# GLA stage of a hybrid decoder layer: queries, keys, decayed keys and outputs turned by VectorE's 32x32 transposes and DMA by way of DRAM instead of TensorE, with head pairs innermost

## The chip, the cores and the metric

The kernel runs on one core of a Trainium2 chip. The metric is the device time of one execution in microseconds. A profile is one execution in which the hardware profiler recorded what each engine did: PE (TensorE; PEld its weight loads), DVE (VectorE), ACT (ScalarE), POOL (GpSimd) and SP, the queue from which this kernel issues its DMAs. Each engine runs its own list of instructions strictly in order and waits on semaphores for the others.

## The reference

One layer over 2048 prompt tokens (and 8x8 sample tokens) of width 1024, in fp32. The change touches the second of its two head groups, gated linear attention (GLA), of 4 heads with keys of 64 and values of 128 columns:

```python
h = rms_norm(x, g_mix_pre)
proj = jnp.einsum('btd,de->bte', h, w_in)
q, k, v, gq, gk, gv, gr, glr = jnp.split(proj, points, axis=-1)
... sliding-window attention of q, k, v -> attn
log_a = log_sigmoid(glr @ w_gk2 + b_gk) / 16          # one decay per token and key column
o, s_new = gla_chunked(gq, gk, gv, log_a, s_init)
o = rms_norm(o, g_gla) * silu(gr)
mix = concat([attn, o]) @ w_out
x = x + rms_norm(mix, g_mix_post)
h = rms_norm(x, g_ffn_pre)
x = x + rms_norm(relu(h @ w_up) ** 2 @ w_down, g_ffn_post)

# gla_chunked, per head, b = running sum of log_a inside a chunk:
#   attn[t, s] = sum_k q[t, k] * 0.125 * exp(b[t, k] - b[s, k]) * k[s, k]     for s <= t
#   o = attn @ v + (q * 0.125 * exp(b)) @ S
#   S = exp(b_last) * S + (k * exp(b_last - b)).T @ v
```

## The kernel before, in words

The program has three parts: the projection and attention of the first head group (to about 308 us), the GLA stage (308 to about 680 us) and the output projection with the MLP (to the end). The change lies in the GLA stage, in `gla(i, gp, og)`, a generator that is run for 16 blocks of 128 tokens. `gp` holds a block's projected queries (columns 0 to 255), keys, values and output gate, tokens on the partitions.

A block is worked off with a hierarchy of levels. For block lengths b of 1 to 64 (`LEVELS`), `before` and `after` hold, with key columns on the partitions and tokens along the free axis, sums of log decays from a sub-block's start and to its end; `level_sums` takes the exponentials for one level (ACT, into `dec`) and then doubles the sub-blocks (two sums on DVE). `weighted` multiplies the left halves' decays with the keys (`XK`) and the right halves' with the queries (`XQ`), on DVE. The matmuls `gl` (levels 0 to 3) and `gh` (levels 4 to 6) take `XK` and `XQ` to the pieces of the attention matrix. `put_level` copies the pieces by mask into `AH` (DVE, COPY_PREDICATED), `put_diagonal` sets the diagonal from the row sums `dg` of queries times keys, and the matrix then stands in `AT`. The state's update is the matmul `ds` of decayed keys `kd` (tokens on the partitions) and values, the state's part of the output the matmuls `o` and `ds` of `qd` and `S`. The `AT` matmuls complete the output of the block.

Key columns must therefore lie on the partitions, while `gp` has tokens there. Four transposes on PE (`gqk`, in `qk_T`) turn queries and keys; a DVE copy (`kt`) and two ACT copies scaled by 0.125 (`qz`, which holds the two heads of a pair in two planes, with zeros in the other head's rows) bring them to SBUF. The decayed keys are computed turned (`kdT`) and brought back by two PE transposes and an ACT copy (`keys_decayed`); in the same PSUM bank, every second block, the low-rank gate input `glr` of two later blocks is turned too. The finished outputs `og` (from `finish_out`: four squares `ojunk` on ACT, a root of the mean `rs_v`, `ors` on DVE and POOL, four products on DVE) are turned by four PE transposes (`ogT`), copied by ACT to `mo` and stored by one DMA to `mix_d`, from where the out projection loads them. The last block's outputs stay in SBUF. Key columns lie as two groups g of 128, group outermost, then tokens.

What sets the order: PE's list is filled with projection matmuls of later blocks (`gproj`, and out-projection matmuls at the end) between the dependent steps; `G_FILL` gives their numbers for the five stretches of a block. `gla` works on the outputs of block i-1 and the decays `z` of block i+1 beside block i. The order on the other engines is fixed when the program is built, by a scheduler that models each engine; `tc.issue_after` adds an edge. So nothing moves aside at run time for an instruction that waits. On SP's list stand also the loads of projection operands (`gxh`, `gxl`), of output-projection weights (`wor`), stores of their split halves (`wo_d` from `wop0`, made on ACT, and `wop1`, made on DVE) and, near the stage's end, loads of these again.

Of the kernel before, what the change touches and what calls it, by code (L numbers as in the profile page):

```python
# [12 lines left out]
F32 = mybir.dt.float32  # L13
# [28 lines left out]
NL = len(LEVELS)  # L42
S_LEVELS = (1, 2, 4)
# [32 lines left out]
G_FILL = (34, 14, 16, 8, 20)  # L76
# [76 lines left out]
def hybrid_step_kernel(ctx: ExitStack, tc: tile.TileContext, I, O):  # L153
# [43 lines left out]
    sm_d = dpool.tile([P, NFC, 2, 2 * NS], F32, name="sm_d")  # L197
    new_d = {name: dpool.tile([NS, P], F32, name=f"new_{name}") for name in "kv"}
# [777 lines left out]
    def log_decays(i, z, t, gt, out):  # L976
        for g in range(2):
            te.matmul(z[:, g], wgk[:, i % 2, g * P : (g + 1) * P], gt[:, : z.shape[2]], start=True, stop=True)
        nc.scalar.activation(t, z, AF.Abs)
        nc.scalar.activation(t, t, AF.Exp, scale=-1.0)  # L980
        if out is not None:
            nc.scalar.activation(out, t, AF.Ln, bias=1.0)
        return z
# [55 lines left out]
    XK = sp.tile([P, NL, 2, P], F32, name="XK")  # L1039
    XQ = sp.tile([P, NL, 2, 2, P // 2], F32, name="XQ")  # L1040
    sgs, prs = places("sg", [P, 512]), places("pr", [P, 256])
    qds = places("qd", [P, 2, P])
    decs = places("dec", [P, NL + 1, 2, P])
    befores, afters = places("before", [P, 2, P]), places("after", [P, 2, P])
    kts = places("kt", [P, 2, P], 2)
    qz = sp.tile([P, 2, 2, P], F32, name="qz")
    zts, kdTs = places("zt", [P, 2, P], 2), places("kdT", [P, 2, P])
# [18 lines left out]
    for u in range(2):  # L1066
        nc.vector.memset(S[u], 0.0)
    nc.gpsimd.memset(qz, 0.0)
# [6 lines left out]
    def decays(i, n, before, kind="d"):  # L1075
# [6 lines left out]
        t = next(zts)[:, :, :n]  # L1082
        if i:
            z = log_decays(i, bank([P, 2, n], kind, f"z_{i}"), t, gt, t)
        else:
            nc.gpsimd.tensor_copy(gt, f32(glrT_first))
            z, e = z0
            nc.scalar.activation(t, e, AF.Ln, bias=1.0)
        nc.vector.scalar_tensor_tensor(before, z, 0.0, t, op0=ALU.min, op1=ALU.subtract)

    def gate(i, gp, n):
# [6 lines left out]
        nc.vector.scalar_tensor_tensor(t[:n], gr, 0.0, t[:n], op0=ALU.min, op1=ALU.subtract)  # L1098
# [4 lines left out]
        engine.tensor_tensor(t4, t4, ggla[:n].unsqueeze(1).to_broadcast([n, 4, P]), op=ALU.mult)  # L1103
        return t

    def qk_T(i, gp, n, kind="d"):
# [6 lines left out]
        kt, q = (next(kts), qz) if n == P else (s_kt, s_qz)  # L1113
        nc.vector.tensor_copy(kt, pt[:, :, 0, :])
        for r, rr in enumerate(half_of):
            nc.scalar.activation(q[rr, r], pt[rr, :, 1, :], AF.Copy, scale=0.125)
        return kt

    def halves(t, b):

        v = t.rearrange("p g (m s b) -> p s g m b", s=2, b=b)
        return v[:, 0], v[:, 1]

    def pairs(t, b, s):
        lead = "p r" if len(t.shape) == 4 else "p"
        t = t.rearrange(f"{lead} g (m s b) -> {lead} (g m) s b", s=2, b=b)
        return t[..., s, :]

    def weighted(xk, xq, dec, kt, q, l, b):
# [4 lines left out]
        out = xq[:, l].rearrange("p r g (m b) -> p r (g m) b", b=b)  # L1134
        nc.vector.tensor_tensor(out, dr.unsqueeze(1).to_broadcast(list(out.shape)), pairs(q, b, 1), op=ALU.mult)

    def keys_decayed(after, kt, kdT, n, kind, kd, pair=0):
# [4 lines left out]
        pk = bank([P, 3, P], kind, f"kdT_{n}")  # L1142
        for g in range(2):
            te.transpose(pk[:n, g, :], kdT[:, g, :], ident)
        ranks = ranks_T(pair, pk[:, 2]) if pair else None
        nc.scalar.activation(kd[:n], pk[:n, :2].rearrange("p g k -> p (g k)"), AF.Copy)
        if pair:
            nc.scalar.activation(glrT[pair % 2], ranks, AF.Copy)

    def level_sums(before, after, dec, l, b):  # L1150
# [3 lines left out]
        left, right = halves(dec[:, l], b)  # L1154
        (bl, br), al = halves(before, b), halves(after, b)[0]
# [3 lines left out]
        nc.vector.tensor_tensor(al, al, br[..., b - 1 :].to_broadcast(list(al.shape)), op=ALU.add)  # L1159
        nc.vector.tensor_tensor(br, br, bl[..., b - 1 :].to_broadcast(list(br.shape)), op=ALU.add)  # L1160

    def put_level(at, gm, mk, b):

        dst = halves(at, b)[1]
# [3 lines left out]
    def put_diagonal(i, at, gp, n):  # L1168

        pr = next(prs)  # L1170
        with tc.issue_after(put[0].ins) if 0 < i < NB else nullcontext():
            nc.vector.scalar_tensor_tensor(pr[:n], gp[:n, 0:256], 0.125, gp[:n, 256:512], op0=ALU.mult, op1=ALU.mult)
# [5 lines left out]
    def finish_out(i, og_src, sg, n, kind):  # L1178
# [3 lines left out]
        for h in range(4):  # L1182
            nc.scalar.activation(junk[:n], og_src(h), AF.Square, accum_out=ssq[:n, h : h + 1])
# [12 lines left out]
        for _ in range(S_WAIT[0] if i == NB else 1):  # L1196
            yield 44, True
        pt = bank([P, 4, P], kind, f"ogT_{i}")
# [11 lines left out]
    def decayed(i):  # L1210

        before, after = next(befores), next(afters)
        yield from decays(i, P, before, "d" if i else "b")
# [3 lines left out]
    def gla(i, gp, og=iter(())):  # L1217
# [6 lines left out]
        kt = qk_T(i, gp, P, "c")  # L1224
        dec = next(decs)
        following = decayed(i + 1) if i < NB - 1 else iter(())
        yield G_FILL[0] + 3 * (i == 1) if i else G_FIRST_FILL, True
        deque(og, 0)
        put_diagonal(i, AH, gp, P)
        for l, b in enumerate(LEVELS):  # L1230
# [5 lines left out]
            if l == NL - 1:  # L1236
                kd = next(kds)
                pair = i // 2 + 1 if i % 2 == 0 and i < NB - 2 else 0
                turned = keys_decayed(after, kt, next(kdTs), P, "e", kd, pair)
                nc.scalar.activation(dec[:, NL], before, AF.Exp, scale=1.0 / 16)  # L1240
            weighted(XK, XQ, dec, kt, qz, l, b)
        next(turned)
# [5 lines left out]
        for r, rr in enumerate(half_of):  # L1248
            nc.vector.tensor_tensor(qd[rr], qz[rr, r], dec[rr, NL], op=ALU.mult)
        yield G_FILL[2], True  # L1250
        deque(turned, 0)
# [6 lines left out]
        for l, gm in enumerate(levels):  # L1258
            for g in range(2):
                keys = XK[:, l, g] if l else kt[:, g]  # L1260
# [1191 lines left out]
```

## Time and profile before

| | |
|---|---|
| median of 3 runs | 2149.47 us (2148.91 to 2149.57) |
| profiled execution | 2150.7 us, span 2148.9 us |
| mean granted TensorE clock | 0.999 |
| busy share PE / DVE / ACT / POOL | 99% / 71% / 57% / 12% |
| `gl` of block 5 to `gl` of block 14 | 191.99 us, nine blocks |

The span is what the profiler saw between the first and the last instruction. Times of instructions are counted in microseconds from its start; rows of the timeline give start, duration, engine, line, operation, output and inputs, and in brackets the idle time before it with what ended it. Buffer numbers are left out of names.

### The profile page before, as it was taken

What the parts mean: (1) busy time and instruction counts of PE and PEld (TensorE: products, weight loads), DVE (VectorE), ACT (ScalarE), POOL (GpSimd) and SP (SyncE); (2) the same over time, 40 slices, a digit from 0 to 9 for tenths busy, and PEclk for the clock granted to TensorE, in tenths of its full rate; (3) what the DMA queues carried; (4) which work ended last, traced back from release to release, by engine and by line L of the source; (5) the groups of instructions that cost most, each with busy time, mean ns of one, the idle gap of its engine ahead of it and who ended that gap; (6) DMA issues with size and microseconds to landing.
All of it is one profiled execution on the core that took longest, in us unless ns stands there. A gap on an engine that the chain in (4) does not pass through costs nothing.

```text
span 2148.9 us, 34602 instructions
## 1 busy us (share of the span) xinstructions
PE 2137.8 (99%) x11974; PEld 1853.1 (86%) x11974; DVE 1530.2 (71%) x3200; ACT 1215.7 (57%) x2627; POOL 261.7 (12%) x422
## 2 busy tenths in 40 slices
PE   9999999999999999999999999999999999999998
PEld 9999999999998888888888888888888888888887
DVE  7999868778875666988887555557776666555566
ACT  7999867566664444655555544345444445544454
POOL 4676511111211110000000000000000000000000
PEclk9999999999999999999999999999999999999999
DMA  7444341243437567777886777668544443766685
GB/s 244 157 145 149 100 118 46 85 144 117 154 112 259 186 221 240 250 261 266 264 276 219 257 240 225 211 201 274 172 171 162 152 161 121 261 202 193 194 274 176
DMA packets 241323, 411.55 MB, mean 192 GB/s; under 512 B 24876, under 2 KB 143132, under 8 KB 237036
## 3 DMA queue, kind: packets, MB, share of 16 engines
q1 hardware_dynamic: 240988, 409.08, 57.6%
q8 instruction: 94, 1.54, 0.3%
q14 instruction: 81, 0.66, 0.1%
q10 hardware_dynamic: 160, 0.27, 0.0%
HBM read 265.82 MB, written 143.99 MB: 191 GB/s over the span
## 4 chain that ended last, share of the span: by engine, by line
PE 92%; DVE 3%; ACT 2%; DMA 1%; issue 1%; POOL 0%; SPq 0%; DVEq 0%; ACTq 0%; POOLq 0%
PE dn L142 28%; PE gproj L142 11%; PE uc L142 8%; PE uX L142 8%; PE out L1432 7%; PE proj L142 6%; PE ue L142 4%; PE ud L142 4%; PE ub L142 4%; PE dsam L142 1%; PE sc L142 1%; PE pT L142 1%; PE sam L142 1%; PE av L142 1%; PE out L142 1%
## 5 line engine op out<-in xcount | busy, mean ns | idle before, releaser
L142 PE MATMUL dn<-o0t,o0s 128*128 128x512 f32 x888 | 345.4, 389 | 0.6 <-DVE f L2090 0.6
L142 PE MATMUL dn<-o1t,o0s 128*128 128x512 f32 x888 | 345.7, 389 | 0.0
L142 PE MATMUL dn<-o0t,o1s 128*128 128x512 f32 x888 | 345.6, 389 | 0.0
L2076 DVE TENSOR_TENSOR o1s<-rs,o0s 128x512 fp32r<-128x512 f32 x224 | 154.5, 691 | 221.5 <-ACT o0s L2075 219.2
L2075 ACT ACTIVATE o0s<-rs 128x512 fp32r<-128x512 f32 x224 | 141.2, 631 | 291.4 <-PE dn L142 255.6
L142 PE MATMUL gproj<-wg,gxh 128*128 128x384 f32 x1024 | 271.1, 341 | 0.0
L142 PEld LDWEIGHTS dn<-o0t,o0s 128*128 128x128 f32 x888 | 166.8, 188 | 37.1 <-DVE f L2090 1.0
L142 ACT ACTIVATE st<-st 128x512 f32<-128x512 f32 x224 | 141.1, 630 | 100.5 <-DVE st L142 95.6
L142 PEld LDWEIGHTS dn<-o1t,o0s 128*128 128x128 f32 x888 | 166.7, 188 | 35.6 <-DVE o1t L2076 0.3
L142 PEld LDWEIGHTS dn<-o0t,o1s 128*128 128x128 f32 x888 | 166.7, 188 | 34.6
L142 PE MATMUL uc<-H,s 128*128 128x512 f32 x768 | 186.5, 391 | 0.1
L142 PEld LDWEIGHTS gproj<-wg,gxh 128*128 128x128 f32 x1024 | 183.8, 188 | 2.4 <-issue 1.9
L142 PE MATMUL gproj<-wg,gxl 128*128 128x384 f32 x576 | 185.9, 340 | 0.0
L142 PE MATMUL uX<-H,w 128*128 128x512 f32 x768 | 185.3, 390 | 0.0
L142 PEld LDWEIGHTS uX<-H,w 128*128 128x128 f32 x768 | 144.0, 188 | 30.4
L142 PEld LDWEIGHTS uc<-H,s 128*128 128x128 f32 x768 | 143.0, 188 | 30.6 <-ACT st L142 0.3
L1432 PE MATMUL out<-wo,mt 128*128 128x512 f32 x680 | 158.6, 392 | 0.0
L218 POOL TENSOR_TENSOR frs<-rs_v,half 128x1 f32<-128x1 f32 (+1 forms) x13 | 12.2, 944 | 1198.5 <-DVE rs_v L216 1198.5
L2076 DVE TENSOR_TENSOR o1t<-rt,o0t 128x512 fp32r<-128x512 f32 x222 | 151.9, 685 | 4.8 <-ACT o0t L2075 4.8
L1432 PEld LDWEIGHTS out<-wo,mt 128*128 128x128 f32 x680 | 126.5, 188 | 26.1
L2075 ACT ACTIVATE o0t<-rt 128x512 fp32r<-128x512 f32 x222 | 137.0, 619 | 8.8 <-DMA rt<-t_d 6.6
L142 DVE TENSOR_TENSOR st<-st 128x512 f32<-128x512 f32 x160 | 110.6, 692 | 31.4 <-ACT st L142 27.1
(444 smaller groups left out, 4314.8 us busy)
## 6 DMA issues: line engine op xcount, KB each, us to landing
s_d<-st SPq DMA_DIRECT2D x32, 1792.0 KB, 8.3
rs<-s_d SPq DMA_DIRECT2D x224, 256.0 KB, 3.6
raw<-in_w_up SPq DMA_DIRECT2D x64, 512.0 KB, 5.0
rt<-t_d SPq DMA_DIRECT2D x128, 256.0 KB, 3.9
rt<-in_w_down SPq DMA_DIRECT2D x96, 256.0 KB, 3.2
t<-in_w_down SPq DMA_DIRECT2D x64, 256.0 KB, 3.8
t_d<-t SPq DMA_DIRECT2D x32, 512.0 KB, 5.5
h_d<-ht SPq DMA_DIRECT2D x8, 1280.0 KB, 7.9
```

What stands on the lines that cost most here:

```text
L142: ins = call(*a, **k)
L218: return nc.gpsimd.tensor_tensor(out, v[:n], e, op=ALU.pow)
L1432: te.matmul(banks[c], x, w[:, c * 512 : (c + 1) * 512], start=k + u == 0, stop=k == KT - 1 and u == len(products) - 1,)
L2075: high = nc.scalar.activation(hi, raw, AF.Copy)
L2076: low = nc.vector.tensor_tensor(lo, raw, f32(hi), op=ALU.subtract)
```

## The change

- **Queries and keys** (`turn`): one DVE transposition of all 512 columns, which turns 32x32 pieces, into `blocks`; four DMAs put these to DRAM (`qk_d`); four DMAs read them back as `kt`, the two planes of `qz`, and an unmasked `qt`. The runs of these DMAs are 64 numbers, 256 bytes.
- **Decayed keys** (`whole`): the last level is no longer doubled (two sums fewer). The whole block's decays `dec[:, NL]` and `kdT` come from the last level's sums, half by half, with the other half's total added as the bias of the exponential (`edge`). `kdT` is turned by DVE, put by four DMAs to `kd_d` and read by one to `kd`. All products of `weighted` are issued behind `whole`.
- **Outputs**: for blocks 0 to 14 one DVE transposition into `mo` and eight DMAs in place of four transposes, a copy and one DMA. Block 15 is as before.
- **Head pairs innermost**: tiles with key columns on the partitions hold the two groups side by side for each token. The operands of `gl`, `gh`, `ds`, `o` and of half of the out projection have a stride of two.
- The factor 0.125 goes into the gain `ggla8` and the square's scale. `qd` is one product instead of two. `kt` has one buffer instead of two.
- The decays `z` of the next block are issued right behind the `AT` matmuls, with the turning of `glr` in their bank; `G_FILL` has 15 for 14, and block 15's first stretch 15 fewer.

```diff
-G_FILL = (34, 14, 16, 8, 20)
+G_FILL = (34, 15, 16, 8, 20)
...
+    def put_blocks(dst, src):
+        for b in range(4):
+            nc.sync.dma_start(dst[b].rearrange("a d x -> d a x"), src[b * 32 : b * 32 + 32].rearrange("d (a x) -> d a x", x=HD))
+
+    def turn(i, gp):
+        with tc.issue_after(put[0].ins) if i else nullcontext():
+            nc.vector.transpose(
+                blocks.rearrange("p (s a t g) -> p s g a t", s=2, a=4, g=2),
+                gp[:, :512].rearrange("p (s g a t) -> p s g a t", s=2, g=2, a=4),
+            )
+        put_blocks(qk_d[i], blocks)
+        q, k = (qk_d[i][:, 4 * u : 4 * u + 4].rearrange("b a d x -> (a d) b x") for u in range(2))
+        for out, src in ((kt, k), *((qz[rr, r], q[rr]) for r, rr in enumerate(half_of)), (qt, q)):
+            nc.sync.dma_start(out.rearrange("p k g -> p (k g)").rearrange("p (b x) -> p b x", b=4), src)
...
+    def whole(i, before, after, dec, kdT, kt, kd):
+        nc.scalar.activation(edge, before[:, HD - 1 :: HD], AF.Copy, scale=1.0 / 16)
+        for u, (out, t) in enumerate(((dec, before), (kdT, after))):
+            src, outs = cut(t, 64), cut(out, 64)
+            nc.scalar.activation(outs[u], src[u], AF.Exp, scale=1.0 / 16)
+            for g in range(2):
+                nc.scalar.activation(
+                    outs[1 - u][..., g], src[1 - u][..., g], AF.Exp, bias=edge[:, u, g : g + 1], scale=1.0 / 16
+                )
+        nc.vector.tensor_tensor(kdT, kdT, kt, op=ALU.mult)
+        nc.vector.transpose(
+            blocks[:, :256].rearrange("p (c i g) -> p g c i", c=4, g=2), kdT.rearrange("p (c t) g -> p g c t", c=4)
+        )
+        put_blocks(kd_d[i], blocks[:, :256])
+        nc.sync.dma_start(kd.rearrange("t (b x) -> t b x", b=4), kd_d[i].rearrange("b c t x -> (c t) b x"))
...
     def finish_out(i, og_src, sg, n, kind):
...
+        if i < NB - 1:
+            mo = next(mos).rearrange("p h t -> p (h t)")
+            nc.vector.transpose(
+                mo.rearrange("p (a q t e) -> p q e a t", a=4, q=2, e=2),
+                og.rearrange("p (q e) (a t) -> p q e a t", e=2, t=32),
+            )
+            for q in range(2):
+                dst = mix_d[i][:, 4 + 2 * q : 6 + 2 * q, :].rearrange("p h t -> p (h t)").rearrange("(a d) x -> d a x", a=4)
+                for c in range(4):
+                    src = mo[c * 32 : c * 32 + 32].rearrange("d (a x) -> d a x", a=4)[:, :, q * HD : (q + 1) * HD]
+                    nc.sync.dma_start(dst[:, :, c * HD : (c + 1) * HD], src)
+            return
...
     def gla(i, gp, og=iter(())):
...
-        kt = qk_T(i, gp, P, "c")
+        turn(i, gp)
         dec = next(decs)
         following = decayed(i + 1) if i < NB - 1 else iter(())
-        yield G_FILL[0] + 3 * (i == 1) if i else G_FIRST_FILL, True
+        next(following, None)
+        yield G_FILL[0] + 3 * (i == 1) - 15 * (i == NB - 1) if i else G_FIRST_FILL, True
...
+        kd = next(kds)
+        whole(i, before, after, dec[:, NL], next(kdTs), kt, kd)
+        for l, b in enumerate(LEVELS):
+            products_of[:] = [weighted(XK, XQ, dec, kt, qz, l, b)]
...
-        for r, rr in enumerate(half_of):
-            nc.vector.tensor_tensor(qd[rr], qz[rr, r], dec[rr, NL], op=ALU.mult)
+        nc.vector.tensor_tensor(qd, qt, dec[:, NL], op=ALU.mult)
```

DVE's list before, in block 8, around the root of the mean of block 7's outputs (`rs_v`) and the outputs `og`. Numbers in names are the block, then a buffer:

```order
L1133 TENSOR_TENSOR XK_4988<-dec0_4993,kt0_4996 128x32x4
L216 TENSOR_SCALAR rs_v_7364<-ossq_7_7357 128x4
L1133 TENSOR_TENSOR XK_4988<-dec0_4993,kt0_4996 128x16x8
L1133 TENSOR_TENSOR XK_4988<-dec0_4993,kt0_4996 128x8x16
L1192 SCALAR_TENSOR_TENSOR og0_4986<-o_7_7297,ors_7_7363,sg0_4990 128x128
```

With the change, the same place:

```order
L1378 SCALAR_TENSOR_TENSOR S0_5009<-S1_5010,dec0_5025,ds_7_7390 128x128 x2
L219 TENSOR_SCALAR rs_v_7462<-ossq_7_7455 128x4
L1268 SCALAR_TENSOR_TENSOR og0_5018<-o_7_7395,ors_7_7461,sg0_5022 128x128
L1268 SCALAR_TENSOR_TENSOR og0_5018<-ds_7_7390,ors_7_7461,sg0_5022 128x128
...
L1107 SCALAR_TENSOR_TENSOR before0_5026<-z_9_7478,zt0_5033 128x256
L1276 STREAM_TRANSPOSE mo0_5019<-og0_5018 128x2x2x4x32
L1230 TENSOR_TENSOR after0_5027<-after0_5027,before0_5026 128x64x2
L1212 TENSOR_TENSOR kdT0_5035<-kdT0_5035,kt_5028 128x256
L1188 TENSOR_TENSOR XK_5020<-dec0_5025,kt_5028 128x32x4
L1213 STREAM_TRANSPOSE blocks_5030<-kdT0_5035 128x2x128
```

The products of keys and decays, which stood on both sides of `rs_v`, stand behind `og`, the transposition of the outputs and `kdT`.

ACT's list before, behind the copies to `AT` of block 9, up to the squares `ojunk` of its outputs (`wop0_4` is a half of split output weights, `gp_10` an eviction of projected columns):

```order
L1287 ACTIVATE AT_4982<-gh_9_7802 64x2x64 x2
L1289 ACTIVATE AT_4982<-AH_4983 64x4x64
L656 ACTIVATE gp_10_7675<-gproj_10_2_7774,rstd_all_183 128x384
L228 ACTIVATE wop0_4_7883<-wor_4_7613 128x1024
L1156 ACTIVATE dec0_4993<-before0_4994 128x8x16
L1158 ACTIVATE dec0_4993<-after0_4995 128x8x16
L1158 ACTIVATE dec0_4993<-after0_4995 128x4x32
L1156 ACTIVATE dec0_4993<-before0_4994 128x4x32
L1158 ACTIVATE dec0_4993<-after0_4995 128x2x64
L1183 ACTIVATE ojunk_9_7890,ossq_9_7889<-o_9_7834 128x128
L1156 ACTIVATE dec0_4993<-before0_4994 128x2x64
L1183 ACTIVATE ojunk_9_7890,ossq_9_7889<-ds_9_7829 128x128
```

With the change, from the same copies (a few exponentials later):

```order
L1374 ACTIVATE AT_5014<-AH_5015 64x4x64
L231 ACTIVATE wop0_4_8003<-wor_4_7725 128x1024
...
L1227 ACTIVATE dec0_5025<-after0_5027 128x128
L1207 ACTIVATE kdT0_5035<-after0_5027 128x128
L1225 ACTIVATE dec0_5025<-before0_5026 128x128
L1204 ACTIVATE edge_5031<-before0_5026 128x4
L1207 ACTIVATE dec0_5025<-before0_5026 128x128
L1209 ACTIVATE kdT0_5035<-after0_5027,edge_5031 128x64 x2
L1209 ACTIVATE dec0_5025<-before0_5026,edge_5031 128x64 x2
L659 ACTIVATE gp_10_7779<-gproj_10_3_7908,rstd_all_215 128x384
L1257 ACTIVATE ojunk_9_8010,ossq_9_8009<-o_9_7950 128x128
L1257 ACTIVATE ojunk_9_8010,ossq_9_8009<-ds_9_7945 128x128
```

The squares moved behind the last level's exponentials, those of `whole` and an eviction.

SP's list before, between the store of `wo_d3` and that of `wo_d4`:

```order
L1449 DMA wor_5_7881<-in_w_out 128x1024
L628 DMA gxh_11_7646<-xt_d11_91 128x1024
L628 DMA gxl_11_7647<-xt_d11_91 128x1024
L1208 DMA mix_d8_71<-mo0_4987 128x512
L1458 DMA wo_d4_151<-wop0_4_7883 128x1024
```

With the change, there (`qk_d9` are the queries and keys of block 9, `mix_d8` the outputs of block 8, `kd_d9` the decayed keys of block 9):

```order
L1131 DMA qk_d9_165<-blocks_5030 32x8x64 x3
L1284 DMA mix_d8_71<-mo0_5019 32x4x64 x3
L1143 DMA kt_5028<-qk_d9_165 128x4x64
L1143 DMA qz_5032<-qk_d9_165 64x4x64 x2
L1143 DMA qt_5029<-qk_d9_165 128x4x64
L1284 DMA mix_d8_71<-mo0_5019 32x4x64 x5
L1131 DMA kd_d9_181<-blocks_5030 32x4x64 x4
L1539 DMA wor_5_8001<-in_w_out 128x1024
L1548 DMA wo_d4_151<-wop0_4_8003 128x1024
L1217 DMA kd1_5017<-kd_d9_181 128x4x64
```

Three of the output puts stand ahead of the read of the keys here, and the store of `wop0_4` ahead of the read of `kd`. Near the end of the stage, SP's list with the change has the reloads of output weights, a gain and `mt_raw` ahead of the eight puts of block 14 and the four of block 15's decayed keys:

```order
L1564 DMA wo1_3_9427<-wo_d7_154 128x512
L1585 DMA wo0_3_9426<-gain_d_190 128x512
L1585 DMA wo1_3_9427<-gain_d_190 128x512
L1589 DMA mt_raw_9450<-mix_d1_64 128x1024
L1284 DMA mix_d14_77<-mo0_5019 32x4x64 x8
L1131 DMA kd_d15_187<-blocks_5030 32x4x64 x4
L1217 DMA kd1_5017<-kd_d15_187 128x4x64
```

More of the change, by code (lines that the diff above doesn't have):

```diff
@@ L42 @@
 NL = len(LEVELS)
+TURNED = (P, P, 2)
 S_LEVELS = (1, 2, 4)
@@ L1141, in keys_decayed @@
         yield
-        pk = bank([P, 3, P], kind, f"kdT_{n}")
+        pk = bank([P, 2, P], "b", "kdT_s")
         for g in range(2):
[L1144 to L1148, printed above, removed]
+            te.transpose(pk[:NS, g, :], kdT[:, g, :], ident)
+        nc.scalar.activation(kd, pk[:NS].rearrange("p g k -> p (g k)"), AF.Copy)
+    def whole(i, before, after, dec, kdT, kt, kd):
[13 more added lines that the diff above has]
+        nc.sync.dma_start(kd.rearrange("t (b x) -> t b x", b=4), kd_d[i].rearrange("b c t x -> (c t) b x"))
     def level_sums(before, after, dec, l, b):
-        left, right = halves(dec[:, l], b)
-        (bl, br), al = halves(before, b), halves(after, b)[0]
+        left, right = cut(dec[:, l], b)
+        (bl, br), al = cut(before, b), cut(after, b)[0]
         nc.scalar.activation(right, br, AF.Exp, scale=1.0 / 16)
@@ L1212, in decayed @@
         before, after = next(befores), next(afters)
-        yield from decays(i, P, before, "d" if i else "b")
+        yield from decays(i, P, before, "c" if i else "b")
         nc.gpsimd.memset(after, 0.0)
@@ L1393, in place_mix, with columns_of @@
         return i, m, ks, raw
+    def columns_of(m, ks, n):
+        turned = m[:, 4:].rearrange("p (q e) t -> p q (e t)", e=2).rearrange("p q (t e) -> p q t e", e=2)
+        return [m[:, k, :n] if k < 4 else turned[:, (k - 4) // 2, :, k % 2] for k in range(ks)]
     def split_mix(i, m, ks, raw, after=None):
```

127 lines of the change are left out of this document (80 added, 47 removed).

## The prediction

> **What bounds the kernel now.** I read the page's head and its chain, then the GLA stage in equal stretches, then the waits there, then one stretch instruction by instruction.
>
> ```profile
> span 2148.9 us, 34602 instructions
> PE 2137.8 (99%) x11974; PEld 1853.1 (86%) x11974; DVE 1530.2 (71%) x3200; ACT 1215.7 (57%) x2627; POOL 261.7 (12%) x422
> ...
> PEclk9999999999999999999999999999999999999999
> ...
> PE 92%; DVE 3%; ACT 2%; DMA 1%; issue 1%; POOL 0%; SPq 0%; DVEq 0%; ACTq 0%; POOLq 0%
> ```
>
> PE is busy for 99% of the span at full granted clock, and the chain lies on it for 92%. In the GLA stage I cut at the starts of the `gl` matmuls of blocks 5 to 14 ("frame k" is from `gl` of block k to that of block k+1):
>
> ```profile
> 486.79:508.07 21.28, 21.28 (x190) 20.62 (x189) 17.23 (x52) 14.26 (x43) 4.03 (x4) 1.00 0.41 137
> ...
> sum 191.99, PE 191.68 PEld 185.05 DVE 153.93 ACT 126.07 POOL 36.29; mean PE 21.30 PEld 20.56 DVE 17.10 ACT 14.01 POOL 4.03
> ```
>
> A frame lasts 21.33 us, PE works 21.30 of it. Its fill of projection matmuls covers everything. The waits (430 to 650 us) tell how much the cover has to spare:
>
> ```profile
> DVE AH L1166 <- PE gl L142: 8.9, 9, 1.9
> DVE og L1192 <- POOL ors L218: 9.1, 11, 0.9
> DVE before L1089 <- ACT zt L982: 8.3, 10, 1.5
> ```
>
> DVE waits for PE's `gl` about 1.0 us in a frame: that is all by which its own loop is shorter than PE's. DVE is busy only 17.1 us, but its fixed order makes it wait for ACT and POOL as well. So what PE is relieved of counts up to 1 us a frame, and beyond that only if DVE's loop gets shorter too.
>
> **PE's gain.**
>
> ```profile
> 404.56 0.60 PE L142 MATMUL gqk<-ident,gp 128*128 128x128 f32 x4
> 404.92 0.60 PE L142 MATMUL gproj<-wg,gxh 128*128 128x384 f32 x2
> ...
> 500.39 0.60 PE L142 MATMUL ogT<-ident,og 128*128 128x128 f32 x4
> 500.74 0.42 PE L142 MATMUL z<-glrT,wgk 128*128 128x128 f32 x2
> ```
>
> Four transposes take 0.36 or 0.35 us start to start, the two of `kdT` half, 0.18. Sixteen blocks lose `gqk` and `kdT`, fifteen lose `ogT`: 16 x 0.54 + 15 x 0.35 = 13.9 us, 0.89 a frame, which leaves PE a frame of 20.4. The fill only moves. The stride-2 operands of `gl`, `gh`, `kd` and `qd` matmuls have no row: from nothing to a doubling of the 2.8 us that these take in a frame (below); I take nothing, as strides on DVE cost nothing (its level sums last 0.29 for every shape of block).
>
> **DVE's loop, frame 7 before.** Time c is the start of the copies from `gl`, 487.99.
>
> ```profile
> 487.99 1.57 DVE L1166 COPY_PREDICATED AH<-c,gl 128x128 f32<-128x128 uint8 x4 [0.99 <-PE gl L142]
> ...
> 492.24 1.23 DVE L229 TENSOR_TENSOR wop<-wor,wop 128x1024 fp32r<-128x1024 f32 x1
> 493.38 0.44 DVE L1176 COPY_PREDICATED AH<-dmsk,dg 128x256 f32<-128x256 uint8 x1
> ...
> 495.30 0.29 DVE L1160 TENSOR_TENSOR before<-before 128x128 f32<-128x128 f32 x1
> ...
> 496.44 0.16 DVE L216 TENSOR_SCALAR rs_v<-ossq 128x4 f32<-128x4 f32 x1
> ...
> 497.90 0.35 DVE L1192 SCALAR_TENSOR_TENSOR og<-o,ors,sg 128x128 f32<-128x128 f32 x1 [0.90 <-POOL ors L218]
> ...
> 498.94 1.75 DVE L1135 TENSOR_TENSOR XQ<-dec,qz 128x256 f32<-128x256 f32 x5
> ...
> 501.90 0.41 DVE L1140 TENSOR_TENSOR kdT<-kdT,kt 128x256 f32<-128x256 f32 x1
> 502.24 0.68 DVE L1098 SCALAR_TENSOR_TENSOR sg<-gp,sg 128x512 f32<-128x512 f32 x1
> 502.84 0.84 DVE L1249 TENSOR_TENSOR qd<-qz,dec 64x256 f32<-64x256 f32 x2
> ...
> 505.30 1.24 DVE L1160 TENSOR_TENSOR before<-before 128x128 f32<-128x128 f32 x1
> ...
> 507.83 0.29 DVE L1160 TENSOR_TENSOR before<-before 128x128 f32<-128x128 f32 x1
> 509.27 1.57 DVE L1166 COPY_PREDICATED AH<-c,gl 128x128 f32<-128x128 uint8 x4 [1.15 <-PE gl L142]
> ```
>
> And ACT in the same frame:
>
> ```profile
> 491.16 1.05 ACT L228 ACTIVATE wop<-wor 128x1024 fp32r<-128x1024 f32 x1
> ...
> 493.01 0.58 ACT L656 ACTIVATE gp<-gproj,rstd_all 128x384 f32<-128x384 f32 x1 [0.61 <-PE gproj L142]
> ...
> 495.55 0.27 ACT L1183 ACTIVATE ojunk<-o 128x128 bf16<-128x128 f32 x1
> ...
> 495.80 0.32 ACT L1156 ACTIVATE dec<-before 128x128 f32<-128x128 f32 x1
> 496.00 0.28 ACT L1183 ACTIVATE ojunk<-ds 128x128 bf16<-128x128 f32 x1
> ```
>
> Busy time hardly changes. DVE loses the `kt` copy (as long as `kdT`, 0.41), one of two `qd` (0.42) and two sums (0.58); it gains transposes of 512, 512 and 256 columns. No row has a DVE transpose: from nothing saved beside a plain pass (0.68, 0.68, 0.42, by `sg` and `kdT`) to twice that; I take the plain pass, 1.78. Net +0.37. ACT loses `mo` and the copies of `qz` and `kd`, and splits two exponentials into six and an edge copy: less work, so not its busy time but its order counts.
>
> That order is frozen. Before, the four squares (`ojunk`) stand among the level exponentials and DVE has key products around `rs_v`, so that it waits 0.90. Now the squares stand behind all exponentials of `whole` and a `gp`, and `rs_v` stands on DVE ahead of `og`, the output transposition, `kdT` and every product. The last level sum ends at c+7.6 (495.59). Behind it ACT has eight exponentials or copies at 0.20 (495.80 to 496.00), `gp` 0.5, two `zt` of twice the width at an estimated 0.3 and four squares at 0.25 (495.55 to 495.80): 3.7 us, `rs_v` at c+11.3 instead of c+8.45, with DVE idle since c+8. Then, by the rows' spacing: `og` at c+12.8 (rs_v to og 1.46), output transposition to c+14.85, `kdT` and its transposition to c+15.9, the products to c+19.3, `sg` and `qd` to c+20.25, and five sums that take turns with ACT's exponentials at 0.40 or 0.2 less where these are not waited for, one of them long by 0.95 (505.30), next copies at c+22.9. A frame with the `wop` split (frames 6 to 12) takes 22.9; without its 1.14 us on DVE (492.24 to 493.38; frames 3, 4, 13), 21.8. Against 20.4 these cost 2.5 and 1.4.
>
> At this place a page of the Trainium skill speaks against the change: "VectorE: DVE Perf Modes", section "The three transpose paths", says that VectorE turns only 32x32 blocks, and "Rules for kernel authors" there sends a 128x128 transpose to TensorE where PSUM can take it. By that page's 311 ns for each 128x128 the ten of a frame would be an estimated 3.1 us rather than my 1.78, and the forecast some 20 us higher. No row here has the operation.
>
> **SP's queue.** One DMA of each block becomes 21.
>
> ```profile
> 502.40 0.32 SPq L1208 DMA_DIRECT2D mix_d<-mo  x1
> ...
> gxh<-xt_d SPq DMA_DIRECT2D x16, 512.0 KB, 4.6
> mix_d<-mo SPq DMA_DIRECT2D x31, 256.0 KB, 2.0
> ...
> q1 hardware_dynamic: 528, 0.13, 65.9%
> ```
>
> Each costs SP 0.32 and lands after 2.0. The last row is 441.9 to 442.8 us: 528 packets of 256 bytes, the size of the new runs, took 0.9 x 0.659 x 16 / 528 = 18 ns each; the 4608 runs of a block make 5.2 us of 16 engines per frame, which lifts their share from 0.41 to about 0.66: hidden. What SP waits for is not:
> (a) In frames 0, 2, 4, 5, 6, 8 and 10 three output puts (one in frame 6) stand ahead of the key read. They wait for DVE's output transposition (c+14.85), so the keys land at 14.85 + 4 x 0.32 + 2.0 = c+18.1, and `kdT` wants them at c+15.05: about +3.0, with nothing else for DVE to do.
> (b) In frames 7, 9 and 11 the `kd` read stands behind the store of `wop0`, which ACT makes only behind that same block's `AT<-gh` copies:
>
> ```profile
> 486.79 0.45 PE L142 MATMUL gl<-XQ,kt 128*64 128x64 f32 x8
> ...
> 488.46 0.61 PE L142 MATMUL ds<-gp,kd 128*64 128x128 f32 x8
> ...
> 489.59 0.62 PE L142 MATMUL gproj<-wg,gxh 128*128 128x384 f32 x2
> ```
>
> `ds` needs `kd` 1.67 us behind `gl`; `wop0` ends at 492.21, 5.42 behind `gl`; two issues and a landing make 8.06. PE stalls 6.4 us, and its frame becomes 20.4 + 6.4 = 26.8. DVE's loop in them, with the squares late by 2.7 since the `AT` matmuls are, is 25.6: PE sets the frame.
> (c) Block 15's `kd` puts stand behind second-half `wo` loads and eight output puts of block 14.
>
> ```profile
> 659.36 0.32 SPq L1208 DMA_DIRECT2D mix_d<-mo  x1
> ...
> 661.34 0.61 PE L142 MATMUL ds<-gp,kd 128*64 128x128 f32 x8
> ```
>
> Eight puts from 659.36 end at 661.9, four more at 663.2, landed 665.2, the read issued and landed 667.5 to 668: `ds` waits about 6.5 us, with only the out projection's matmuls behind it on PE.
>
> **The sum**, idle PE by frame: 7, 9, 11: 3 x 6.4 = 19.2; 5, 6, 8, 10 (split and late keys; frame 5 lasts 21.8 + 3.0 at least, I count it with them) 4 x 5.5 = 22.0; 4 (late keys) 4.4; 12: 2.5; 3 and 13: 2.8; 0 and 2, half of 4.4 each since sample work stretches these frames anyway, 4.4; block 15: 6.5. Together 61.8. The profiled execution took 2150.7 (span 2148.9, 1.8 around it), 1.2 above the median: 2150.7 - 13.9 + 61.8 = 2198.6, or 2197 against the median. This measurement tells differences from about 0.2% (4.3 us).
>
> **The rivals.**
> Keys in time: reads are early enough in (a), since a wait I put on SP is met sooner or DVE's lateness overlaps it. Frames 5, 6, 8, 10 then cost 2.5, frame 4 1.4, 0 and 2 0.7 each: 43.8 in all, 2179. For it: a landing of 2.0 leaves 5 us between keys transposed at c+6.5 and wanted at c+15; against: the order of the queue.
> PE still the bound but for (b) and (c): DVE's idle time before `rs_v` is taken up by PE's slack, because the exponentials need fewer than 3.7 us. Then -13.9 + 19.2 + 6.5: 2161. For it: DVE's busy time is 17.5 of 20.4.
> Faster: the above, and the `kd` reads come in time in frames 7, 9, 11. Place: SP ahead of that read. It decides when the stall is under (13.9 - 6.5)/3 = 2.5 us instead of 6.4, which needs `wop0` ready about 1.5 us behind `gl`; at no stall 2142, without (c) as well 2136. Against: `wop0` follows `AT<-gh` on ACT. For: strides and transposes could also be cheaper than I see.
> PE slowed by its own waits: stalls of 5 to 6 us do not occur before, where the granted clock is 1.00 throughout. If PE ran at half speed for as long as one of the three stalls and (c) lasted, 4 x 3 us: 2209. The Trainium skill, "TensorE: Matmul & The Clock Gate", section "What's actually happening", says the clock halves after an idle window of some 3.4 us; no row of before can show that.
>
> **How the numbers follow.** Forecast with late keys 0.33, keys in time 0.20, PE-bound but for SP 0.17, slowed clock 0.08; no change, where the last two cancel, 0.05; faster 0.17. So 2197 is the single likeliest; the range leaves out only the faster case and reaches to 2210 for slow clock or dear transposes, and below to 2147. Its own range, for slower alone, is 2155 to 2210. Faster 0.17, same 0.05, slower 0.78.
>
> **What would show it.** PE idle at `ds` for `kd` about 6 us in frames 7, 9, 11 and block 15 shows (b) and (c); DVE idle at `kdT` for a DMA of `kt` shows (a); DVE's wait of 3 us at `rs_v` for `ojunk` the new order; `gl` 20.4 us apart in frames without either shows the gain. I am wrong if DVE still waits for PE's `gl` at each block, if transposes take much over 0.68 us, or if `gl` matmuls lengthen.

## The result, and the profile after

The changed kernel takes 2254.56 us (median of 4 runs, 2250.97 to 2258.70) against 2149.52: 1.049 times as long, 95% interval 1.0469 to 1.051. It got slower by 105 us where 47 were forecast, and lies above the range. The profiled execution spans 2254.9 us. Of its page:

```profile
span 2254.9 us, 34691 instructions
PE 2153.0 (95%) x11818; PEld 1860.1 (82%) x11818; DVE 1536.8 (68%) x3183; ACT 1206.0 (53%) x2644; POOL 259.4 (12%) x423
...
PEclk9999999998899899999999999999999999999999
...
PE 84%; DVE 6%; DMA 5%; ACT 2%; issue 1%; SPq 1%; POOL 0%; DVEq 0%; POOLq 0%; ACTq 0%
```

PE stands still for 101.9 us instead of 11.1, and is busy 15.2 us longer although 13.9 us of work were taken from it. Of these 29 us about 3 are operands with a stride of two (2.3 us in the out projection, see e12, and about 1 in the GLA stage); the rest, some 26 us, I put down to matmuls at a lower granted clock. 90.8 us more of standing still and 15.2 us more of work are the 106 us between the spans. The frames (from `gl` of a block to that of the next) are now unlike each other:

```profile
556.22:579.04 22.82, 20.93 (x180) 19.79 (x180) 11.99 (x38) 12.09 (x40) 1.32 (x2) 1.00 0.49 135
579.04:614.45 35.41, 24.13 (x181) 22.60 (x181) 23.25 (x64) 15.12 (x49) 6.44 (x6) 0.81 0.48 130
```

Columns as before: start and end, length, busy time of PE, PEld, DVE, ACT and POOL, granted clock, DMA share, GB/s. Frame 8 is 1.6 us longer than before, frame 9 13.9 us. By `gl` starts the 106 us are: ahead of block 0's `gl` 9.6; frames 1, 3, 5 25.5; frames 7, 9, 11 39.6; the other nine 9.3; behind block 15's `gl` 22.1. The waits from 300 to 800 us (total, times, longest):

```profile
PE ds L143 <- DMA kd<-kd_d: 66.8, 9, 18.1
...
DVE rs_v L219 <- ACT ojunk L1257: 54.3, 15, 7.8
...
DVE kdT L1212 <- DMA kt<-qk_d: 34.6, 11, 5.2
```

PE waits 66.8 us for decayed keys to come back from DRAM: 4.6, 6.0 and 3.2 in frames 1, 3, 5, 1.6 in frame 6, 10.0, 10.5, 10.1 in 7, 9, 11, 2.8 in 14 and 18.1 in block 15. Frames 8 and 9 in the timeline, all engines:

```profile
557.45 1.59 DVE L1237 COPY_PREDICATED AH<-c,gl 128x128 f32<-128x128 uint8 x4 [0.96 <-PE gl L143]
...
560.13 0.71 DVE L1136 STREAM_TRANSPOSE blocks<-gp 128x512 f32<-128x512 f32 x1
...
569.07 0.17 DVE L219 TENSOR_SCALAR rs_v<-ossq 128x4 f32<-128x4 f32 x1 [4.00 <-ACT ojunk L1257]
...
571.74 0.70 DVE L1276 STREAM_TRANSPOSE mo<-og 128x512 f32<-128x512 f32 x1
...
572.47 1.25 SPq L1284 DMA_DIRECT2D mix_d<-mo  x3
574.21 0.75 SPq L1143 DMA_DIRECT2D kt<-qk_d  x1
...
576.84 0.43 DVE L1212 TENSOR_TENSOR kdT<-kdT,kt 128x256 f32<-128x256 f32 x1 [4.23 <-DMA kt<-qk_d]
...
577.39 0.44 DVE L1213 STREAM_TRANSPOSE blocks<-kdT 128x256 f32<-128x256 f32 x1
...
582.01 0.43 DVE L1237 COPY_PREDICATED AH<-c,gl 128x128 f32<-128x128 uint8 x1
...
587.18 1.04 ACT L231 ACTIVATE wop<-wor 128x1024 fp32r<-128x1024 f32 x1
588.25 0.34 SPq L1548 DMA_DIRECT2D wo_d<-wop  x1
588.78 0.37 SPq L1217 DMA_DIRECT2D kd<-kd_d  x1
...
592.12 1.12 PE L143 MATMUL ds<-gp,kd 128*64 128x128 f32 x8 [10.47 <-DMA kd<-kd_d]
...
594.73 0.84 PE L143 MATMUL gproj<-wg,gxh 128*128 128x384 f32 x2
595.37 0.52 PE L143 MATMUL gproj<-wg,gxl 128*128 128x384 f32 x1
...
598.35 0.51 PE L143 MATMUL gproj<-wg,gxh 128*128 128x384 f32 x2
598.70 0.34 PE L143 MATMUL gproj<-wg,gxl 128*128 128x384 f32 x1
```

`rs_v` comes 11.6 us behind the copies (forecast 11.3), the output transposition ends at 572.4, 15.0 behind (14.85), and DVE then waits 4.23 us for keys whose read stands behind three output puts. PE goes on with `gl`, but DVE's copies start late, at 582.01, and stand among level sums; so `wop0` ends at 588.2, 9.2 us behind `gl`, its store is issued, then the read of `kd`, and `ds` starts at 592.12. Behind that wait PE runs at half clock until 598.2: two `gproj` take 0.64 us from start to start, and 0.35 from then on.

### The profile page after: what moved, and what is told of

Its sections match the earlier page's. It is cut to its first block, busy times and chain, and to the rows that moved or that the text cites. A ratio compares the mean times of both kernels' runs of the same rounds, so it can differ in the third digit from the quotient of the medians.

```text
span 2254.9 us, 34691 instructions
## 1 busy us (share of the span) xinstructions
PE 2153.0 (95%) x11818; PEld 1860.1 (82%) x11818; DVE 1536.8 (68%) x3183; ACT 1206.0 (53%) x2644; POOL 259.4 (12%) x423
## 4 chain that ended last, share of the span: by engine, by line
PE 84%; DVE 6%; DMA 5%; ACT 2%; issue 1%; SPq 1%; POOL 0%; DVEq 0%; POOLq 0%; ACTq 0%
PE dn L143 25%; PE uc L143 8%; PE uX L143 8%; PE gproj L143 7%; PE out L1522 7%; PE proj L143 6%; PE ud L143 4%; PE ue L143 4%; PE ub L143 4%; PE sam L143 2%; PE dsam L143 1%; PE sc L143 1%; PE pT L143 1%; PE av L143 1%; DMA kd<-kd_d 1%
## 5 line engine op out<-in xcount | busy, mean ns | idle before, releaser
L143 PE MATMUL gproj<-wg,gxh 128*128 128x384 f32 x1024 | 277.9, 350 | 0.3 <-ACT gp L659 0.3
L143 PEld LDWEIGHTS gproj<-wg,gxh 128*128 128x128 f32 x1024 | 194.1, 197 | 1.8 <-ACT gp L659 0.9
L143 PE MATMUL gproj<-wg,gxl 128*128 128x384 f32 x576 | 191.4, 350 | 0.0
L1522 PE MATMUL out<-wo,mt 128*128 128x512 f32 x680 | 160.9, 395 | 0.0
L2165 ACT ACTIVATE o0t<-rt 128x512 fp32r<-128x512 f32 x222 | 137.3, 619 | 10.8 <-DMA rt<-t_d 4.4
L143 DVE TENSOR_TENSOR st<-st 128x512 f32<-128x512 f32 x160 | 110.7, 692 | 30.6 <-ACT st L143 26.2
```

Of the source, the lines that this page charges most:

```text
L143: ins = call(*a, **k)
L1522: te.matmul(banks[c], x, w[:, c * 512 : (c + 1) * 512], start=k + u == 0, stop=k == KT - 1 and u == len(products) - 1,)
L2165: high = nc.scalar.activation(hi, raw, AF.Copy)
```

## The experiments

Theory 1: the round trip of `kd` by DRAM, late on SP, holds PE at `ds`, and the low clock follows. Rival: the new order on ACT and DVE makes DVE's loop the bound, and the stalls lie beside it. Runs without an interval are one profiled execution each, against 2150.0 to 2150.6 of the kernel before beside them; the four executions of the changed kernel lie up to 7.7 us apart. "By PE" means turned by TensorE, as before the change.

**e1: `kd` by PE.**

```diff
-        nc.vector.transpose(blocks[:, :256]..., kdT...)
-        put_blocks(kd_d[i], blocks[:, :256])
-        nc.sync.dma_start(kd..., kd_d[i]...)
+        yield                                   # resumed behind G_FILL[2]
+        pk = bank([P, 2, P], "e", f"kdT_{i}")
+        for g in range(2):
+            te.transpose(pk[:, g, :], kdT[:, :, g], ident)
+        nc.scalar.activation(kd.rearrange("t (k g) -> t g k", g=2), pk, AF.Copy)
```

> The changed kernel, but decayed keys brought back by two transposes on PE and one ACT copy per block, as before; queries, keys and outputs still go by DVE and DRAM. Theory 1 (PE's stall at ds for kd and the low clock that follows are the cost): the 67 us idle at ds go, and most of the 29 us by which PE got slower; 2.9 us of PE come back: about 2165 to 2178, with no wait at ds over 1 us. Rival (ACT's and DVE's order makes DVE's loop the bound, and the stalls at ds lie beside it): frames stay at 22.9 us or more without the stalls, 2190 to 2215, with DVE's wait for the squares unchanged and PE idle ahead of gl.

It took 2191.59 us. The stalls at `ds` are gone and 63 us with them, so theory 1 has the larger part; but the time is above both of that theory's bounds and lies in the rival's range (2190 to 2215). The rival's signs are missing: DVE's wait for the squares fell from 54.3 to 17.6 us, and frames 6, 8 and 12 last 20.54 us. What is left lies elsewhere: PE now waits at another place, the turning of `glr`: 3.6, 2.5, 2.8 and 2.9 us in frames 3, 5, 9, 11, and still 6.1 at block 1's `z`.

**e2: SP's order.**

```diff
+                    with tc.issue_after(read[0].ins):        # the last read of keys and queries
                         nc.sync.dma_start(dst[:, :, c * HD : (c + 1) * HD], src)
...
+                with tc.issue_after(kd_read[0].ins):
                     nc.sync.dma_start(wo_d[k][:, u], f32(parts[u]))
```

> The changed kernel with nothing but SP's order changed: output puts stand behind the reads of the next block's keys and queries, and the stores of the split output weights behind the read of kd. If the order of the queue is the cost (my steps a and b): the stalls at ds of 10 us in frames 7, 9 and 11 become 1 to 3.5 us, kdT waits for kt under 1 us: about 2205 to 2220. If the round trip by DRAM is too long in any order: stalls of 3 us or more in all frames, 2225 or more. Block 15's stall of 18 us and block 0's stay in both.

It took 2254.45 us, no change. There are still three long stalls at `ds`, of 11.1, 9.9 and 10.8 us (frames 6, 7 and 9), and in frame 5 `kdT` still waits 4.2 us for `kt`: by the profile SP now waits for the puts of queries and keys to land (3.6 us). The store of the split weights had gone from ahead of the read, but the load of the next output weights (`wor`) still stood there, and it waits for the same split, since it takes over its buffer. The run does not decide; e8 takes up the question.

**e3: block 1's `z` behind block 0's fill.**

```diff
-        next(following, None)
+        if i:
+            next(following, None)
```

> The changed kernel, with the decay matmuls z of block 1 behind block 0's fill, as before, and not ahead of it; all other blocks unchanged. PE waits 6.05 us there for a cast on POOL that stands behind memsets, and runs at 0.85 clock around it: 9 us less if this is a cost of its own, 2244 to 2247; if later frames absorb it, within 3 us of the changed kernel.

It took 2251.18 us, 3.4 us less, which is within the spread of the changed kernel; the trace tells more. Block 0's `gl` starts 4.7 us earlier instead of 9: the wait at `z` went, one of 3.5 us at the turning of `glr` right behind it came.

**e4: layout and order only**: e1's edit, and queries, keys and outputs by PE too.

> All three turned by PE again, as before; what stays of the change is head pairs innermost (strides of two at the matmuls), the last level's sums left out, whole() with products behind it, z early. If the layout costs PE nothing (as I forecast): gl, gh and ds take the 1.67 us of before, and the time is that of before plus block 0's 9 us, 2149 to 2165. If strided operands cost: gl to ds takes up to 3.3 us, and the time is up to 45 us longer, 2170 to 2195.

It took 2197.90 us: 47 us slower than before without any of the new DMAs or DVE transposes. But the strides are not it: `gl` to `ds` takes 1.73 us instead of 1.67. From frame 5 to frame 11 the odd frames have 26.2 to 26.3 us, the even ones 21.4 to 22.2, and an odd one shows why:

```profile
522.53 0.42 PE L143 MATMUL z<-glrT,wgk 128*128 128x128 f32 x2
525.90 0.33 PE L143 MATMUL z<-ident,glr 128*128 128x128 f32 x1 [2.96 <-ACT zt L984]
...
525.46 0.38 ACT L984 ACTIVATE zt<-z 128x256 f32<-128x256 f32 x1
...
527.31 0.85 PE L143 MATMUL gproj<-wg,gxh 128*128 128x384 f32 x2
```

`glr` is turned into the bank of `z` and therefore waits until ACT has read `z`, for which ACT takes its turn behind the squares; PE's list has no fill between the two. The 3 us and the half clock behind them cost 4.7 to 6.1 us in each of the six odd frames up to 11; ahead of block 0's `gl` another 10 us are lost, where PE waits 5.5 us for the POOL cast of e3. I had written this move down and given it no price.

**e5: e4, with `glr` turned ahead of `z`, and e3's edit.**

```diff
+            ranks = ranks_T(pair, pz[:, 2]) if pair else None
             z = log_decays(i, pz[:, :2], t, gt, t)
             if pair:
-                nc.scalar.activation(glrT[pair % 2], ranks_T(pair, pz[:, 2]), AF.Copy)
+                nc.scalar.activation(glrT[pair % 2], ranks, AF.Copy)
```

> As e4 (all three turned by PE, layout and order of the change kept), but the turning of glr stands ahead of the z matmuls in their bank, so that it need not wait for ACT's read of z, and block 1's z behind block 0's fill. Theory 1b (e4's 47 us are PE's 3 us waits for ACT at that place, seven times, with the half clock behind each, plus block 0; strided operands cost nothing): 2149 to 2156, frames of 21.2 to 21.5, clock 0.999. Rival (the new order or the strides cost part of it): 2165 or more with frames above 22.

It took 2161.79 us, 1.0052 times before (1.0036 to 1.0068). 36 of the 47 us are gone; what is left lies between the two theories: plain frames of 21.4 against 21.2 to 21.3 before, and a low clock in two frames (0.93 in 2 and 14, 1.8 us each).

**e6: e1 with the same two repairs** (e1's diff and those of e3 and e5).

> As e1 (kd by PE; queries, keys and outputs by DVE and DRAM), with the same two repairs. If the stalls at z explain what is left of e1: 2191 less 7 x 4.8 less 5 is 2153, and 10.9 us of PE work stay removed: 2145 to 2156. If DVE's loop (squares behind whole, 22.9 us) is what is left: frames of 22.5 to 24.5 without a stall of PE at z, 2165 to 2185.

It took 2173.48 us, 1.0111 times before (1.0093 to 1.0129), inside the second range. PE does not wait at `z`, frames 6 to 13 have 22.0 to 24.5 us, and DVE waits for `kt` (19.4 us in ten frames). Here the rival is right: in frames 8 to 11 PE is busy for 21.1 to 21.6 us of 22.1 to 24.5.

**e7: the changed kernel with the two repairs alone** (the diffs of e3 and e5).

> The changed kernel with only those two repairs; kd still by DRAM. In the changed kernel PE waits at z for ACT 1.4 us at most, since the stall at ds ahead of it has let ACT catch up: if so, nothing is won in frames 3 to 14, 2245 to 2252 by block 0 alone. If the two stalls add up instead: 2220 or less.

It took 2245.85 us, as expected: the stalls at `ds` (9.1, 10.3 and 9.1 us in frames 7, 9 and 11) had covered the one at `glr`. From e7 to e6 only `kd` differs: 72 us.

**e8: e2 with the repairs, and `wor` too behind the read of `kd`**.

```diff
-        with tc.issue_after(done.ins):
+        with tc.issue_after(done.ins), tc.issue_after(kd_read[0].ins):
             next(wo_parts, None)
```

> e2 with the two repairs and with the loads of output weights (wor), which e2 left ahead of the kd read waiting for DVE's split, behind that read as well; everything still by DVE and DRAM. If SP's order alone makes the 10 us stalls: no stall at ds over 3.5 us in frames 1 to 13, 2185 to 2210, with block 15's 17 us left. If the round trip itself is too long: stalls of 3 to 5 us at ds in nearly every frame, 2215 to 2240.

It took 2219.16 us, 27 us less than e7. The stalls in frames 7, 9 and 11 shrink to 0.4, 2.9 and 4.2 us; frames 8 and 10 get new ones of 2.5 and 2.7; those of frame 1 (5.2) and block 15 (17.2) stay. Order made 5 to 9 us of each long stall. What is left is in the second range, but it does not show a round trip that is too long in any order. In frames 6 to 11 the eight output puts, moved behind the reads of the keys, now stand ahead of the puts of `kd`, which begin 3.1 to 4.4 us behind DVE's transposition, as in frame 10:

```profile
575.66 3.84 SPq L1286 DMA_DIRECT2D mix_d<-mo  x8
...
576.08 0.44 DVE L1214 STREAM_TRANSPOSE blocks<-kdT 128x256 f32<-128x256 f32 x1
...
579.60 1.80 SPq L1132 DMA_DIRECT2D kd_d<-blocks  x4
...
582.66 0.38 SPq L1218 DMA_DIRECT2D kd<-kd_d  x1
...
585.58 0.66 PE L143 MATMUL ds<-gp,kd 128*64 128x128 f32 x8 [2.65 <-DMA kd<-kd_d]
```

**e9: e7 with `kd`'s five DMAs on POOL's queue**, and POOL's products for the gate behind them, so that nothing stands ahead.

```diff
-        put_blocks(kd_d[i], blocks[:, :256])
-        nc.sync.dma_start(kd..., kd_d[i]...)
+        put_blocks(kd_d[i], blocks[:, :256], nc.gpsimd)
+        kd_read[:] = [nc.gpsimd.dma_start(kd..., kd_d[i]...)]
```

> e7 with the four puts and the read of kd issued by POOL instead of SP (POOL's gate products behind the read); everything else, the round trip by DRAM included, unchanged. If the stalls at ds come from what stands ahead of kd on SP: they shrink from 9 to 10 us to under 3 in frames 7, 9, 11, and block 15's from 17.9 to under 4: 2185 to 2205. If the round trip is too long by itself: stalls of 3 to 6 us in nearly every frame, 2215 or more.

It took 2233.79 us, the second case by its time. Block 15's stall falls from 17.9 to 9.5 us, but `ds` waits 1.9 to 6.1 us in twelve of the fifteen frames, as in frame 10:

```profile
594.65 0.44 DVE L1215 STREAM_TRANSPOSE blocks<-kdT 128x256 f32<-128x256 f32 x1
...
595.38 2.25 POOL L1133 DMA_DIRECT2D kd_d<-blocks  x4 [7.07 <-DVE blocks L1215]
601.41 0.77 POOL L1219 DMA_DIRECT2D kd<-kd_d  x1 [3.77 <-ACT dec L1229]
...
604.02 1.12 PE L143 MATMUL ds<-gp,kd 128*64 128x128 f32 x8 [3.71 <-DMA kd<-kd_d]
```

From the end of the transposition (595.1) to `ds` pass 8.9 us with nothing ahead on the queue: puts, landing, read, landing. PE would be ready for `ds` 5.2 us behind that transposition, since only the products and `gl` and `gh` lie between. But these 8.9 us are the price on POOL's queue, and SP's is lower: from the first put's issue to `ds` pass 8.3 to 9.5 us in frames 8 to 11 here, and 5.4 to 6.0 in the same frames of e8; in block 0, where neither queue holds anything ahead of the puts, 7.0 here and 5.2 in e8. In frame 10 the four puts take 2.25 us for 1.80 on SP, and the read begins 3.8 us behind them for 1.3; why, no run shows. So the run shows that POOL's queue does not cure the stalls, not that the round trip is too long on SP. In the changed kernel PE is ready 3.8 to 5.3 us behind the transposition in frames 1, 3, 5, 7, 9 and 11; by SP's 5.2 to 6.0 us, less these, my estimate is that up to 2.2 us of each stall would stay with nothing ahead. No run has tried that.

**e10: e5 with the outputs by DVE and DRAM.**

```diff
-        if False:                      # e5: all outputs by PE
+        if i < NB - 1:                 # as in the changed kernel
```

> e5 (layout, glr ahead), with only the outputs by DVE and DRAM; queries, keys and kd by PE. PE loses 15 x 0.35 = 5.2 us against e5, DVE gains 0.65 us a frame, within its slack of about 1 us: 2156 to 2160 if the slack covers it; 2161 to 2167 if it does not.

It took 2156.00 us, 1.0027 times before (1.0017 to 1.0037) and 5.8 us less than e5: this part pays, by PE's 5.2 us and a little more. Its frames:

```profile
514.92:535.98 21.06, 21.06 (x187) 20.37 (x186) 18.36 (x51) 14.31 (x47) 4.06 (x4) 1.00 0.45 138
```

**e11: e5 with queries and keys by DVE and DRAM**, as in the changed kernel.

```diff
-        pt = bank([P, 2, 2, P], "c", f"gqk_{i}")
-        ...
+        nc.vector.transpose(blocks..., gp[:, :512]...)
+        put_blocks(qk_d[i], blocks)
+        ...
+            nc.sync.dma_start(out..., src)
```

> e5 with only queries and keys by DVE and DRAM; kd and outputs by PE. PE loses 16 x 0.36 = 5.8 us against e5. No output put stands ahead of the key read here: 2156 to 2161 if the landing of the keys is then early enough; 2166 to 2175, most of e6's 11.7 over e5, if DVE still waits for kt by 1 to 3 us a frame, as in e6.

It took 2194.52 us, 1.0207 times before (1.019 to 1.0224), 33 us more than e5 and worse than either expectation. DVE waits 43.1 us for `kt` in eleven frames, and PE then for `kdT`:

```profile
545.45 0.34 SPq L1303 DMA_DIRECT2D mix_d<-mo  x1
545.83 0.43 SPq L1549 DMA_DIRECT2D wor<-in_w_out  x1
546.44 0.37 SPq L1144 DMA_DIRECT2D kt<-qk_d  x1
...
550.85 0.43 DVE L1213 TENSOR_TENSOR kdT<-kdT,kt 128x256 f32<-128x256 f32 x1 [4.50 <-DMA kt<-qk_d]
```

The one wide output store that is left stands ahead of the key read, and waits for ACT's copy; the 512 KB load is ahead too, and the keys arrive 4.4 us behind the issue of their read.

**e12: the kernel before with the outputs by DVE alone**, its layout and order untouched.

```diff
+        if i < NB - 1:
+            mo = next(mos).rearrange("p h t -> p (h t)")
+            nc.vector.transpose(mo..., og...)
+            ...
+                    nc.sync.dma_start(dst[:, :, c * HD : (c + 1) * HD], src)
+            return
...
+            return [columns_of(m[:, u], ks, n) for u in (1, 2)]   # the out projection's stride
```

> The kernel before with one part of the change alone: outputs of blocks 0 to 14 by one DVE transposition and eight puts (and the stride of two in the out projection that goes with them); layout, keys, kd, z and the order of the rest as before. e10 won 5.8 us over e5 by this part. Here PE loses 5.2 us and DVE gains 0.65 us a frame against a slack of 1.0: 2144 to 2147, faster than both kernels, if frames shrink to 20.9; 2148 to 2152 if DVE's loop takes the gain back.

It took 2152.56 us against 2150.47, 1.0008 times (0.9999 to 1.0017): no change that can be told. Block 15's `gl` starts 2.0 us earlier (657.70 instead of 659.67). Of the 5.2 us that PE no longer has to work, 3.2 are lost by then, 2.1 of them at `ds`, which waits 3.0 us for ACT's copy of `kd` (0.9 before). The out projection, whose operands now have a stride of two in half its steps, gives back the other 2.0. Its row in the pages of before and after (total busy us, mean ns of one, idle ahead); e12's has the same 160.9:

```profile
L1432 PE MATMUL out<-wo,mt 128*128 128x512 f32 x680 | 158.6, 392 | 0.0
```

```profile
L1522 PE MATMUL out<-wo,mt 128*128 128x512 f32 x680 | 160.9, 395 | 0.0
```

160.9 us of PE for 158.6 before: 2.3 us. In the two profiled executions 1.5 us more are lost behind block 15's `gl`, for a reason that stays open. No version that was run beats the kernel before.

Undone one after the other, the parts cost: 2254.6 as changed; repairs of `z` and `glr` 2245.9; `kd` by PE 2173.5; queries and keys by PE 2156.0; layout and order as before 2152.6; outputs as before 2150. What a part costs depends on the others: queries and keys cost 17 us with the outputs by DVE (e6 against e10), 33 with the outputs by PE (e11 against e5).

## Why the prediction was wrong

The direction, the queue's waits and DVE's order were right; the waits of PE at `ds` were too small, since waits were added where they make each other longer, and three costs had no term in the sum. The waits in four even frames were too large, which hid 13.5 us of the miss.

- **PE's gain** (0.35 for the outputs, 13.9 in all): e10's plain frames are 0.36 shorter than e5's. For queries, keys and outputs together e1's plain frames are 0.64 shorter than before (20.54 for 21.18), which is 0.71 less 0.07 for strides. Right.
- **Strides**, taken as nothing: 0.07 us a frame at `gl` to the next fill (2.87 for 2.80), 2.3 us in the out projection, which I had left out of that term. Small.
- **DVE's transposes**, taken as 0.68, 0.68, 0.42: 0.71, 0.70, 0.44. Right. The 311 ns (of bf16) for each 128x128 in the Trainium skill ("VectorE: DVE Perf Modes", "The three transpose paths") would have made four of them 1.24 us by estimate; the trace, at 0.70 to 0.71 in fp32, does not agree. Its rule to use TensorE was still the better advice for the decayed keys (72 us, e7 against e6) and for queries and keys (17 us), for a reason that it does not give: the 32x32 pieces make a round trip by DRAM to be put together, and a consumer waits for it. For the outputs, which no step of the next blocks needs, DVE paid in e10.
- **Order on ACT and DVE**: `rs_v` and the output transposition of frame 8 came within 0.3 us of my hand calculation. But I had DVE's five level sums ahead of the next copies in every frame; in the odd frames they stand among and behind them, so that `gl` need not wait for them: frame 4, for which I forecast 24.8, has 20.9, and frames 6, 8 and 10, for which I forecast 25.9, have 22.1 to 23.2. In nine blocks DVE still waits for PE's `gl` (9.1 us in all), which I had named as a sign of being wrong: there PE, not DVE's loop, sets the frame.
- **(a) late keys**: the wait is there (4.23 where I said 3.0), but not paid in its own frame. It makes the copies late, hence `wop0`, hence `kd` in the next.
- **(b)**, 6.4 us in three frames: 10.0 to 10.5. This is the step that failed: I took `wop0` at its old place, 5.4 us behind `gl`, with everything else in time; it ended 7.9 to 9.2 us behind. Of the 3.8 us in frame 9, 1.8 are the late copies and 2.0 the level sums among them. And I looked for stalls at `ds` only in these three frames and block 15; in frames 1, 3, 5, 6 and 14 `kd` came late too, 18 us in all, since the round trip (5.2 to 6.0 us in e8 from the first put) began too late or was held up.
- **(c)** block 15, 6.5 us: 18.1. I started the eight puts where the one store had stood, 0.3 us ahead of `gl`; they came 8.8 us behind it, since reads of keys now stand ahead of the weight reloads, and eight of them took 5.5 us, not 2.6.
- **Block 0**, 9.6 us: `z` ahead of the fill waits for a POOL cast behind memsets. It had no term.
- **`z` and `glr`**: no term either; 36 us when nothing else covers it (e4 against e5, with block 0), 9 in the changed kernel (e7).
- **Low clock**: a rival at 0.08 and 12 us. It came with every wait of PE of 4.5 us or more and with some shorter ones, and cost about 26. It should have been a term of every case with waits of several microseconds.

What stays open: why e11's single store leaves the keys later than e6's eight puts do is read from SP's list, not tried; no run took away the low clock while keeping the waits; and no run gave `kd`'s puts and read an SP queue with nothing ahead, so what the round trip alone costs there is an estimate.

## What to carry to other kernels

A transposition by way of memory is not a cost in busy time but a latency of puts, landing, read and landing (here 5.2 to 6.0 us on SP's queue once the puts are issued, 7.0 to 9.5 on POOL's, in the frames compared above); set it against the shortest work between its producer and its consumer, and against what stands ahead of it on an in-order queue, with the frame already late. Waits in an in-order program make each other longer: after one is found, recompute the times of all others from the delayed frame, and allow for the low clock behind waits of 2 us and more, which here brought it in some cases and not in others. An instruction moved to another bank or place inherits that place's readers; give every such move a price, however small it looks.

## What the hardware showed

The half clock came in stretches of 3.4 us or a whole multiple of it: 3.4 us behind waits of PE of 2.10 us (e5, frame 14) and 2.96 us (e4), and 13.7 us around the wait of 10.47 us (changed kernel, 584.5 to 598.2, so 6.1 us of it behind the wait; a `gproj` took 0.32 us from start to start instead of 0.17). The length of the one wait does not decide alone. Waits of 3.16 and 2.83 us (frames 5 and 14 of the changed kernel) and of 1.96 us (e6) left the clock at 1.00, and in frame 2 of e5 it was half for 3.4 us although the longest wait just ahead was 0.81 us, among the small matmuls of the sample tokens. The Trainium skill, "TensorE: Matmul & The Clock Gate", "What's actually happening", puts the drop after an idle window of about 3.4 us that runs freely; the length of the slow stretches agrees, but waits well under it were enough.

A put of 32 partitions with several runs each occupied SP for 0.30 to 0.70 us (median 0.43 for the outputs and `kd`), the plain store of the kernel before for 0.32; plain reloads of weights that follow one another also have a median of 0.43, so it is not shown that the shape of the put is what costs. On POOL's queue the same puts took 0.55 us each (e9).
